# Row-wise largest magnitude of an 8192 x 8192 matrix: 64 adjacent rows per partition and one store at the end

## The chip, the cores and the metric

One core of one Trainium2 chip runs the kernel. The metric is the device time of one execution in microseconds (us), lower is better. Repeated executions of the kernel before agree within 0.2%. Every timed comparison below uses fast runs (granted clock 1.0); single runs, whose state is unknown, are called that. Ratios are computed as the mean time of one kernel's fast runs over that of the other's of the same rounds, so they are not quite the ratio of the medians that are quoted.

## The reference

```python
def setup_inputs():
    return {"x": np.random.randn(8192, 8192).astype(np.float32)}   # 268.44 MB

def reference(x):
    return np.linalg.norm(x, ord=np.inf, axis=1)   # max |x| of each row, 8192 results
```

Each element is read once and takes part in one maximum. There is nothing to reuse, so the kernel is a stream of loads with a reduction behind it.

## The kernel before

The 8192 rows are dealt out to 128 partitions, 64 rows each, in 32 tiles of two rows per partition (8 MB a tile, 64 KB per partition). The first 24 tiles, the bulk, are each one load and one reduction on the vector engine (DVE). The last 8 tiles, the tail, are loaded in ever shorter column pieces, so that DVE can follow closely and little work is left after the last byte. A list fixes the pieces. Three tile buffers rotate; all loads are issued by SyncE (SP), on one queue.

```python
TAIL = [ [2944, 13440], [4096, 12288], [11520, 4864], [7680, 8704],   # columns of float32
    [6528, 3328, 6528], [4864, 4096, 3328, 4096], [3968, 3584, 3328, 2944, 2560],
    [2432, 2176, 1920, 1664, 1536, 1280, 1152, 1024, 1152, 1024, 1024] ]
# ... (cut: bookkeeping, and a hook that issues the first load early)
# G=4, B=2, P=128, A=6, W=2*8192; split = 6144 rows
x_b = x[:split].rearrange("(a p n b) c -> a n p (b c)", p=P, a=A, n=G, b=B)
out_b = out[:split].rearrange("(a p n b) -> p a (n b)", p=P, a=A, n=G, b=B)
x_t = x[split:].rearrange("(p t b) c -> t p (b c)", p=P, b=B)
out_t = out[split:].rearrange("(p t) -> p t", p=P)
# ...
for a in range(A):
    for n in range(G):
        t = sbuf.tile([P, W + PAD], F32, tag="t")
        nc.sync.dma_start(out=t[:, :W], in_=x_b[a, n])
        absmax(r_bulk[:, a, n*B:(n+1)*B], t[:, :W].rearrange("p (b c) -> p b c", b=B))
nc.scalar.dma_start(out=out_b, in_=r_bulk[:])          # early store of the bulk's results
# ... tail: one load per piece from x_t[i][:, at:at+w], one or two reductions per piece
nc.scalar.dma_start(out=out_t[:, :n_tail-1], in_=r_tail[:, :n_tail-1])   # near the end
# ...
nc.sync.dma_start(out=out_t[:, n_tail-1:], in_=r_fin[:])                 # last row
```

The distance in memory between what neighbouring partitions read for one tile is called the pitch. A row is 32 KB. In the bulk a partition owns G*B = 8 adjacent rows, so the pitch is 256 KB. In the tail it owns 16, so it is 512 KB. The contiguous piece that one partition reads in one load is called the run: 64 KB in the bulk, 52.5 KB down to 4 KB in the tail. In the trace each run is one packet, moved by one of the 16 DMA engines; a load lands when its last packet has arrived.

Of the kernel before, what the change touches and what calls it, by code (L numbers as in the profile page):

```python
# [1 line left out]
logging.getLogger("concourse").setLevel(logging.ERROR)  # L3

# [1 line left out]

# [4 lines left out]

F32 = mybir.dt.float32
X = mybir.AxisListType.X



TAIL = [
    [2944, 13440],
    [4096, 12288],
    [11520, 4864],  # L20
    [7680, 8704],
    [6528, 3328, 6528],
    [4864, 4096, 3328, 4096],
    [3968, 3584, 3328, 2944, 2560],
    [2432, 2176, 1920, 1664, 1536, 1280, 1152, 1024, 1152, 1024, 1024],
]


def segments(loads, cols):

    out, at = [], 0
    for i, w in enumerate(loads):
        end = at + w
        while at < end:
            r = at // cols
            to = min(end, (r + 1) * cols)
            out.append((i, r, at - r * cols, to - at))
            at = to
    return out


def start_first_load_early(nc):


    sp = mybir.EngineType.SP
    first, *rest = nc.main_func.blocks
    for block in rest:
        insts = block.instructions
        for i, ins in enumerate(insts):
            if ins.engine == sp and type(ins).__name__ == "InstDMACopy":  # L50
                assert not ins.sync_info.on_wait
                moved = insts[i]
                block.instructions = insts[:i] + insts[i + 1 :]
                head = first.instructions
                at = next(k for k, h in enumerate(head) if h.engine == sp)
                first.instructions = head[:at] + [moved] + head[at:]
                return


@with_exitstack  # L60
def kernel(
    ctx: ExitStack,
    tc: tile.TileContext,
    x: bass.AP,
    out: bass.AP,
    G: int = 4,
    B: int = 2,
    BUFS: int = 3,
    PAD: int = 16,
):  # L70
    nc = tc.nc
    P = nc.NUM_PARTITIONS
    rows, cols = x.shape
    W = B * cols


    n_tail = B * len(TAIL)
    n_bulk_rows = rows // P - n_tail
    assert n_bulk_rows % (G * B) == 0
    A = n_bulk_rows // (G * B)  # L80
    split = n_bulk_rows * P
    x_b = x[:split].rearrange("(a p n b) c -> a n p (b c)", p=P, a=A, n=G, b=B)
    out_b = out[:split].rearrange("(a p n b) -> p a (n b)", p=P, a=A, n=G, b=B)
    x_t = x[split:].rearrange("(p t b) c -> t p (b c)", p=P, b=B)
    out_t = out[split:].rearrange("(p t) -> p t", p=P)

    sbuf = ctx.enter_context(tc.tile_pool(name="sbuf", bufs=BUFS))
    outp = ctx.enter_context(tc.tile_pool(name="outp", bufs=1))

    segs = [segments(loads, cols) for loads in TAIL]  # L90
    count = {}
    for i, s in enumerate(segs):
        for _, r, _, _ in s:
            count[i * B + r] = count.get(i * B + r, 0) + 1
    n_last = count[n_tail - 1]
    k_max = max(count[r] for r in range(n_tail - 1))
    assert n_last - 1 <= PAD

    r_bulk = outp.tile([P, A, G * B], F32)
    r_tail = outp.tile([P, n_tail], F32)  # L100
    r_fin = outp.tile([P, 1], F32)
    part = outp.tile([P, n_tail - 1, k_max], F32)
    nc.vector.memset(part[:], 0.0)  # L103

    def absmax(o, i):
        nc.vector.reduce_max(out=o, in_=i, axis=X, apply_absolute_value=True)  # L106

    for a in range(A):
        for n in range(G):
            t = sbuf.tile([P, W + PAD], F32, tag="t")  # L110
            nc.sync.dma_start(out=t[:, :W], in_=x_b[a, n])
            absmax(
                r_bulk[:, a, n * B : (n + 1) * B],
                t[:, :W].rearrange("p (b c) -> p b c", b=B),
            )
    nc.scalar.dma_start(out=out_b, in_=r_bulk[:])

    seen = {}
    for i, loads in enumerate(TAIL):
        t = sbuf.tile([P, W + PAD], F32, tag="t")  # L120
        todo = segs[i]
        at = 0
        for j, w in enumerate(loads):
            nc.sync.dma_start(out=t[:, at : at + w], in_=x_t[i][:, at : at + w])  # L124
            at += w
            for _, b, c, n in [s for s in todo if s[0] == j]:
                r = i * B + b
                k = seen.get(r, 0)
                seen[r] = k + 1
                lo = b * cols + c  # L130
                if r < n_tail - 1:
                    absmax(part[:, r, k : k + 1], t[:, lo : lo + n])
                    if r == n_tail - 2 and k == count[r] - 1:

                        absmax(r_tail[:, : n_tail - 1], part[:])
                        nc.scalar.dma_start(
                            out=out_t[:, : n_tail - 1], in_=r_tail[:, : n_tail - 1]
                        )
                elif k < n_last - 1:
                    absmax(t[:, W + k : W + k + 1], t[:, lo : lo + n])  # L140
                else:

                    absmax(r_fin[:], t[:, lo : W + n_last - 1])
    nc.sync.dma_start(out=out_t[:, n_tail - 1 :], in_=r_fin[:])
    nc.at_finalize(start_first_load_early)


# [1 line left out]
_INS = ['x']  # L149
_OUTS = [((8192,), 'float32')]  # L150


# [23 lines left out]
```

## Time and profile before

| | before |
|---|---|
| time | 628.59 us, median of 3 runs (628.57 to 628.78) |
| load queue | 99.3% of the 16 DMA engines' span, 268.44 MB |
| DVE | 553.0 us busy, 88% |
| last reduction starts | 623.80 us |

The page of the kernel before, its 40 slices and its queue table (packets, MB, share of the engines' span):

```profile
DVE  0688998888988889888898888998889999999998
...
DMA  9999999999999999999999999999999999999997
GB/s 401 468 401 468 401 468 401 464 405 455 414 451 418 451 418 401 468 401 468 401 468 401 468 401 468 401 468 401 468 418 406 460 430 410 436 422 430 428 423 287
...
q1 hardware_dynamic: 8064, 268.44, 99.3%
```

The DMA engines are busy in every slice but the last. The swing between 401 and 468 is only how long packets fall into slices; the windows view of the same kernel (stretch, its length, DVE busy time with instruction count, POOL, clock, DMA share, GB/s), in five stages, is flat in the bulk:

```profile
0.00:80.00 80.00, 51.80 (x5) 0.20 (x4) 1.00 1.01 433
80.00:480.00 400.00, 357.21 (x21) 0.00 (x0) 1.00 1.00 433
480.00:560.00 80.00, 79.28 (x14) 0.00 (x0) 1.00 0.99 426
560.00:600.00 40.00, 39.77 (x13) 0.00 (x0) 1.00 1.00 425
600.00:627.00 27.00, 24.95 (x15) 0.00 (x0) 1.00 0.84 350
```

The packet records in the trace say the same more sharply. A 64 KB packet nearly always takes 2.418 us, 27.1 GB/s on each of 16 engines, 434 GB/s in all. The Trainium skill, "DMA: Bandwidth & Descriptors", section "Where 436 GB/s comes from", gives 435.2 GB/s as the ceiling of the engines' ports; this trace agrees. Only the first 16 packets, which all start together, average 2.98 us.

The timeline of DVE in the kernel before (start, duration, what, and in brackets the idle time before it and what ended it):

```profile
21.93 17.22 DVE L106 TENSOR_REDUCE r_bulk<-t 128x2 f32<-128x16384 f32 x1 [20.95 <-DMA t<-in_x_dram]
41.22 17.22 DVE L106 TENSOR_REDUCE r_bulk<-t 128x2 f32<-128x16384 f32 x1 [2.07 <-DMA t<-in_x_dram]
60.58 17.22 DVE L106 TENSOR_REDUCE r_bulk<-t 128x2 f32<-128x16384 f32 x1 [2.14 <-DMA t<-in_x_dram]
...
615.73 0.22 DVE L106 TENSOR_REDUCE r_tail<-part 128x15 f32<-128x60 f32 x1
615.86 7.90 DVE L106 TENSOR_REDUCE t<-t 128x1 f32<-128x1536 f32 x6
623.80 1.23 DVE L106 TENSOR_REDUCE r_fin<-t 128x1 f32<-128x1030 f32 x1
```

In the bulk a tile arrives every 19.35 us, DVE needs 17.22 us for it and waits about 2 us for the next. In the tail DVE has a single gap, of 0.64 us. The start of each bulk reduction is therefore a clock for the loads: comparing it between two kernels shows where a loss arises. That is the main instrument below.

### The profile page before, as it was taken

Reading aid. Unit: us, or ns where it says so; the run is one execution under the profiler, and the core shown is the slowest. Engines: PE = TensorE matmul, PEld = TensorE weight load, DVE = VectorE, ACT = ScalarE, POOL = GpSimd, SP = SyncE. Lnnn points to the kernel's source line nnn. Section 1 sums busy time; section 2 is a strip of 40 time slices with the busy share of each in tenths; the row PEclk is TensorE's granted clock in tenths of the full one; section 3 lists DMA queues with packets and bytes.
Section 4 is the critical chain, followed back from the end, with each engine's and each line's share of the span. In section 5 each row is a group of like instructions: output and inputs, shape, how many; then the busy total and the mean of one; then the engine's idle time right before and its main releaser. Section 6 shows DMA issues by size and latency. Waiting matters only on the chain.

```text
span 627.3 us, 201 instructions
## 1 busy us (share of the span) xinstructions
DVE 553.0 (88%) x64; POOL 0.2 (0%) x4
## 2 busy tenths in 40 slices
DVE  0688998888988889888898888998889999999998
POOL 0000000000000000000000000000000000000000
DMA  9999999999999999999999999999999999999997
GB/s 401 468 401 468 401 468 401 464 405 455 414 451 418 451 418 401 468 401 468 401 468 401 468 401 468 401 468 401 468 418 406 460 430 410 436 422 430 428 423 287
DMA packets 8994, 268.49 MB, mean 428 GB/s; under 512 B 1952, under 2 KB 1952, under 8 KB 3104
## 3 DMA queue, kind: packets, MB, share of 16 engines
q1 hardware_dynamic: 8064, 268.44, 99.3%
q10 hardware_dynamic: 928, 0.03, 0.1%
q14 instruction: 2, 0.02, 0.0%
HBM read 268.44 MB, written 0.03 MB: 428 GB/s over the span
## 4 chain that ended last, share of the span: by engine, by line
DMA 67%; DVE 28%; another core or an unknown queue 4%; SPq 0%; issue 0%
DMA t<-in_x_dram 67%; DVE r_bulk L106 22%; DVE part L106 5%; DVE t L106 1%; DVE r_fin L106 0%; SPq L124 0%; DVE r_tail L106 0%
## 5 line engine op out<-in xcount | busy, mean ns | idle before, releaser
L106 DVE TENSOR_REDUCE r_bulk<-t 128x2 f32<-128x16384 f32 x24 | 413.3, 17220 | 70.1 <-DMA t<-in_x_dram 70.1
L106 DVE TENSOR_REDUCE part<-t 128x1 f32<-128x8192 f32 (+18 forms) x31 | 130.5, 4273 | 0.9 <-DMA t<-in_x_dram 0.6
L106 DVE TENSOR_REDUCE t<-t 128x1 f32<-128x1152 f32 (+3 forms) x6 | 7.9, 1387 | 0.0
L106 DVE TENSOR_REDUCE r_fin<-t 128x1 f32<-128x1030 f32 x1 | 1.2, 1226 | 0.0
L103 DVE MEMSET part<- 128x60 f32 x1 | 0.1, 108 | 0.9 <-PEq L160 0.9
L106 DVE TENSOR_REDUCE r_tail<-part 128x15 f32<-128x60 f32 x1 | 0.2, 216 | 0.0
L160 POOL MEMSET const-bfloat16-1.0<- 128x1 bf16 x1 | 0.1, 103 | 0.0
L160 POOL MEMSET const-uint8-127<- 128x1 uint8 x1 | 0.1, 103 | 0.0
L160 POOL MEMSET const-float32-1.0<- 128x1 f32 x1 | 0.1, 100 | 0.0
L160 POOL MEMSET const-float32-0.0<- 128x1 f32 x1 | 0.1, 99 | 0.2 <-issue 0.2
## 6 DMA issues: line engine op xcount, KB each, us to landing
t<-in_x_dram SPq DMA_DIRECT2D x1, 6720.0 KB, 40.4
t<-in_x_dram SPq DMA_DIRECT2D x2, 3264.0 KB, 26.4
t<-in_x_dram SPq DMA_DIRECT2D x3, 2048.0 KB, 29.0
t<-in_x_dram SPq DMA_DIRECT2D x1, 6144.0 KB, 40.6
t<-in_x_dram SPq DMA_DIRECT2D x1, 5760.0 KB, 35.3
t<-in_x_dram SPq DMA_DIRECT2D x3, 1664.0 KB, 32.5
t<-in_x_dram SPq DMA_DIRECT2D x2, 2432.0 KB, 32.6
t<-in_x_dram SPq DMA_DIRECT2D x1, 4352.0 KB, 42.8
```

The lines of the kernel that those rows point to most:

```text
L103: nc.vector.memset(part[:], 0.0)
L106: nc.vector.reduce_max(out=o, in_=i, axis=X, apply_absolute_value=True)
L160: nc = _bacc.Bacc("TRN2", target_bir_lowering=False, num_devices=1)
```

## The change

The intent is a simpler layout: every partition holds 64 adjacent rows throughout, so bulk and tail share one view, and each partition's 64 results are contiguous in the output. One store of 256-byte runs replaces three stores of short runs (768 of 32 bytes, 128 of 60, 128 of 4). The same rearrangement sets the pitch to 64 x 32 KB = 2 MB everywhere. Loads, their sizes and their order, and the reductions stay as they were.

```diff
-    x_b = x[:split].rearrange("(a p n b) c -> a n p (b c)", p=P, a=A, n=G, b=B)
-    out_b = out[:split].rearrange("(a p n b) -> p a (n b)", p=P, a=A, n=G, b=B)
-    x_t = x[split:].rearrange("(p t b) c -> t p (b c)", p=P, b=B)
-    out_t = out[split:].rearrange("(p t) -> p t", p=P)
+    x_v = x.rearrange("(p t b) c -> t p (b c)", p=P, b=B)
+    out_v = out.rearrange("(p t) -> p t", p=P)
 ...
-    r_bulk = outp.tile([P, A, G * B], F32)
-    r_tail = outp.tile([P, n_tail], F32)
-    r_fin = outp.tile([P, 1], F32)
+    res = outp.tile([P, n_rows], F32)
 ...
-            nc.sync.dma_start(out=t[:, :W], in_=x_b[a, n])
+        nc.sync.dma_start(out=t[:, :W], in_=x_v[i])
 ...
-    nc.scalar.dma_start(out=out_b, in_=r_bulk[:])
 ...
-            nc.sync.dma_start(out=t[:, at : at + w], in_=x_t[i][:, at : at + w])
+            nc.sync.dma_start(out=t[:, at : at + w], in_=x_v[n_bulk + i][:, at : at + w])
 ...
-                        nc.scalar.dma_start(out=out_t[:, : n_tail - 1], in_=r_tail[:, : n_tail - 1])
 ...
-    nc.sync.dma_start(out=out_t[:, n_tail - 1 :], in_=r_fin[:])
+    nc.sync.dma_start(out=out_v, in_=res[:])
```

More of the change, by code (lines that the diff above doesn't have):

```diff
@@ L65 @@
     out: bass.AP,
-    G: int = 4,
     B: int = 2,
@@ L74 @@
     W = B * cols
-    n_tail = B * len(TAIL)
-    n_bulk_rows = rows // P - n_tail
-    assert n_bulk_rows % (G * B) == 0
-    A = n_bulk_rows // (G * B)
-    split = n_bulk_rows * P
-    x_b = x[:split].rearrange("(a p n b) c -> a n p (b c)", p=P, a=A, n=G, b=B)
-    out_b = out[:split].rearrange("(a p n b) -> p a (n b)", p=P, a=A, n=G, b=B)
-    x_t = x[split:].rearrange("(p t b) c -> t p (b c)", p=P, b=B)
-    out_t = out[split:].rearrange("(p t) -> p t", p=P)
+    n_rows = rows // P
+    n_bulk = n_rows // B - len(TAIL)
+    first = n_bulk * B
+    last = n_rows - 1
+    x_v = x.rearrange("(p t b) c -> t p (b c)", p=P, b=B)
+    out_v = out.rearrange("(p t) -> p t", p=P)
     sbuf = ctx.enter_context(tc.tile_pool(name="sbuf", bufs=BUFS))
@@ L93 @@
         for _, r, _, _ in s:
-            count[i * B + r] = count.get(i * B + r, 0) + 1
-    n_last = count[n_tail - 1]
-    k_max = max(count[r] for r in range(n_tail - 1))
+            r += first + i * B
+            count[r] = count.get(r, 0) + 1
+    n_last = count[last]
+    k_max = max(n for r, n in count.items() if r < last)
     assert n_last - 1 <= PAD
-    r_bulk = outp.tile([P, A, G * B], F32)
-    r_tail = outp.tile([P, n_tail], F32)
-    r_fin = outp.tile([P, 1], F32)
-    part = outp.tile([P, n_tail - 1, k_max], F32)
+    res = outp.tile([P, n_rows], F32)
+    part = outp.tile([P, last - first, k_max], F32)
     nc.vector.memset(part[:], 0.0)
@@ L106, in absmax @@
         nc.vector.reduce_max(out=o, in_=i, axis=X, apply_absolute_value=True)
-    for a in range(A):
-        for n in range(G):
-            t = sbuf.tile([P, W + PAD], F32, tag="t")
-            nc.sync.dma_start(out=t[:, :W], in_=x_b[a, n])
-            absmax(
-                r_bulk[:, a, n * B : (n + 1) * B],
-                t[:, :W].rearrange("p (b c) -> p b c", b=B),
-            )
-    nc.scalar.dma_start(out=out_b, in_=r_bulk[:])
+    for i in range(n_bulk):
+        t = sbuf.tile([P, W + PAD], F32, tag="t")
+        nc.sync.dma_start(out=t[:, :W], in_=x_v[i])
+        absmax(
+            res[:, i * B : (i + 1) * B],
+            t[:, :W].rearrange("p (b c) -> p b c", b=B),
+        )
     seen = {}
@@ L123 @@
         for j, w in enumerate(loads):
-            nc.sync.dma_start(out=t[:, at : at + w], in_=x_t[i][:, at : at + w])
+            nc.sync.dma_start(
+                out=t[:, at : at + w], in_=x_v[n_bulk + i][:, at : at + w]
+            )
             at += w
             for _, b, c, n in [s for s in todo if s[0] == j]:
-                r = i * B + b
+                r = first + i * B + b
                 k = seen.get(r, 0)
@@ L130 @@
                 lo = b * cols + c
-                if r < n_tail - 1:
-                    absmax(part[:, r, k : k + 1], t[:, lo : lo + n])
-                    if r == n_tail - 2 and k == count[r] - 1:
-                        absmax(r_tail[:, : n_tail - 1], part[:])
-                        nc.scalar.dma_start(
-                            out=out_t[:, : n_tail - 1], in_=r_tail[:, : n_tail - 1]
-                        )
+                if r < last:
+                    absmax(part[:, r - first, k : k + 1], t[:, lo : lo + n])
+                    if r == last - 1 and k == count[r] - 1:
+                        absmax(res[:, first:last], part[:])
                 elif k < n_last - 1:
@@ L141 @@
                 else:
-                    absmax(r_fin[:], t[:, lo : W + n_last - 1])
-    nc.sync.dma_start(out=out_t[:, n_tail - 1 :], in_=r_fin[:])
+                    absmax(res[:, last:], t[:, lo : W + n_last - 1])
+    nc.sync.dma_start(out=out_v, in_=res[:])
     nc.at_finalize(start_first_load_early)
```

## The prediction

> **What bounds the kernel now.** DMA: the page shows 9 tenths busy in every slice but the last; its queue table gives the load queue 99.3% of the 16 DMA engines' span for 268.44 MB, 428 GB/s. The windows view reads 434 GB/s, DMA share 1.00, from 100 to 460 us. In the trace's packet records nearly every 65,536-byte load packet takes 2.42 us (27.1 GB/s per engine), as flat as an engine at its own limit, not at memory's. DVE is second: 17.22 us per 8 MB tile (groups by form), against about 19.3 us of DMA (half the period in the chain of waits). In the bulk DVE idles 70 us, all on loads; from 506 us to the end at 625 it runs without a gap.
>
> **What changes on the engines.** The order comparison shows the same DVE instructions, shapes and loads. Removed: two ACT stores (768 runs of 32 bytes, 128 of 60 bytes). The last store grows from 128 runs of 4 bytes to 128 of 256.
> - In 500:560, where the bulk store trickles, loads run at 425 instead of 434 GB/s: at most 1.2 us of DMA time (estimate: 2% of 60 us). DVE has no gap there and sets the end, so I credit under 0.5 us.
> - Last store: 1.4 us to landing now (issues table). A 256-byte run at 27 GB/s is about 10 ns, 8 per engine: below +0.3 us (estimate).
> - Alone this is a draw.
>
> **What moves: the address.** A bulk tile's partitions were 256 KB apart, the tail's 512 KB; now all are 2 MB apart. Tail packets of 46 and 54 KB still run at 27.1 GB/s per engine: no loss at 512 KB. The Trainium skill, "DMA: Bandwidth & Descriptors", section "Latency and other measured facts", row on HBM row pitch, gives copies of 128-partition tiles 207 GB/s per direction at a 512 KiB pitch, 164 at 2 MiB, 103 at 4 MiB, and guesses at channel aliasing of lock-stepped streams. No run here shows that yet. Those were copies with 16 KB rows; this is loads alone with 64 KB rows, so the loss may be smaller, or vanish when engines drift apart.
>
> **On the critical path:** all of it. Estimate from that page: 616 us of transfer (268.44 MB at 435 GB/s) times 207/164 is 778 us, plus start and end of about 10: 788. DVE then waits for each load, so its backlog at the end (about 5 us after the last landing) shrinks to about 1.5 us. I take three quarters of the effect: load packets average about 2.9 us.
>
> **Predicted: 745 us, 80% range 627 to 835. Faster by over 2%: 0.02; within 2%: 0.21; slower: 0.77.** Two humps: near 628 (no aliasing) and 680 to 820.
>
> **What would show it.** Right: 64 KB load packets longer than 2.42 us and uneven; load rate 340 to 400 GB/s at DMA share 1.0; DVE busy time still 553 us with far larger idle on loads, in the tail too; loads in the bulk landing after about 48 us instead of 40.7; DVE's last reduction within about 2 us of the last landing; last store about 1.5 us.
> Wrong: packets stay at 2.42 us; then the time is 628 within 1 us.
>
> **What would make it wrong.** Engines that drift apart after the first packets (here the first 16 take about 2.9 us, later ones 2.42) and so never meet on one memory channel; aliasing that hits stores more than loads; or a much stronger loss for loads alone, beyond 835.

## The result, and the profile after

| | before | after |
|---|---|---|
| time, median of 5 runs | 628.68 us (628.57 to 629.10) | 654.73 us (652.79 to 655.43) |
| ratio of fast runs | | 1.0407, 95% interval 1.0389 to 1.0424 |
| DVE busy | 553.0 us | 554.2 us |
| last reduction starts | 623.80 us | 647.98 us |

The changed kernel is slower by 26 us. That lies inside the stated range, in the gap between its two humps, but the forecast was a loss of about 117 us. The page of the changed kernel, the same lines:

```profile
DVE  0479888889888889988888988888989999999856
...
DMA  9999999999999999999999999999999999999994
GB/s 370 342 414 427 427 431 435 447 422 435 431 451 414 439 435 447 418 435 439 447 418 427 447 431 427 435 447 427 417 438 433 428 425 430 409 413 405 346 242 142
...
q1 hardware_dynamic: 8064, 268.47, 98.6%
```

The rate is low in the first two slices and in the last four, and as good as before between. DMA stays busy all the while, so it is the packets that take longer. The windows view of the changed kernel, by the same stages:

```profile
0.00:80.00 80.00, 46.48 (x4) 0.20 (x4) 1.00 0.99 395
80.00:480.00 400.00, 354.67 (x22) 0.00 (x0) 1.00 1.00 433
480.00:560.00 80.00, 79.22 (x13) 0.00 (x0) 1.00 1.00 429
560.00:600.00 40.00, 39.03 (x11) 0.00 (x0) 1.00 1.00 412
600.00:650.00 50.00, 34.78 (x18) 0.00 (x0) 1.00 0.86 256
```

The timeline of DVE in the changed kernel, at its start and end:

```profile
25.95 17.22 DVE L102 TENSOR_REDUCE res<-t 128x2 f32<-128x16384 f32 x1 [24.97 <-DMA t<-in_x_dram]
47.96 17.22 DVE L102 TENSOR_REDUCE res<-t 128x2 f32<-128x16384 f32 x1 [4.79 <-DMA t<-in_x_dram]
68.07 17.22 DVE L102 TENSOR_REDUCE res<-t 128x2 f32<-128x16384 f32 x1 [2.89 <-DMA t<-in_x_dram]
...
621.78 2.69 DVE L102 TENSOR_REDUCE part<-t 128x1 f32<-128x2432 f32 x1 [2.49 <-DMA t<-in_x_dram]
626.75 2.42 DVE L102 TENSOR_REDUCE part<-t 128x1 f32<-128x2176 f32 x1 [2.28 <-DMA t<-in_x_dram]
...
647.98 1.23 DVE L102 TENSOR_REDUCE res<-t 128x1 f32<-128x1030 f32 x1
```

Subtract the starts of the reductions before from those after: +4.0, +6.7, +7.5, +7.8 us for the first four, then 7.3 to 7.9 for the other twenty. The last reduction is +24.2. So the start loses 7.9 us in four tiles, the remaining bulk loses nothing at the same 2 MB pitch, and the tail loses 16.3 us (24.2 minus 7.9). The mean of the 64 KB packets, tile by tile, is 2.89, 2.66, 2.50, 2.43 us and then 2.42.

The stores cost nothing that shows: the last store is issued at 625.05 and 649.23 us, and the spans end 2.3 us later both times.

Two things are to be explained: why the 2 MB pitch costs at the start and then stops, and why it costs again in the tail.

### The profile page after: what moved, and what is told of

Its sections match the earlier page's. It is cut to its first block, busy times and chain, and to the rows that moved or that the text cites. A ratio compares the mean times of both kernels' runs of the same rounds, so it can differ in the third digit from the quotient of the medians.

```text
span 651.5 us, 197 instructions
## 1 busy us (share of the span) xinstructions
DVE 554.2 (85%) x64; POOL 0.2 (0%) x4
## 3 DMA queue, kind: packets, MB, share of 16 engines
HBM read 268.44 MB, written 0.03 MB: 412 GB/s over the span
## 4 chain that ended last, share of the span: by engine, by line
DMA 72%; DVE 27%; another core or an unknown queue 0%; issue 0%; SPq 0%
DMA t<-in_x_dram 72%; DVE res L102 24%; DVE part L102 3%; DVE t L102 0%; SPq L118 0%
## 5 line engine op out<-in xcount | busy, mean ns | idle before, releaser
L102 DVE TENSOR_REDUCE res<-t 128x2 f32<-128x16384 f32 (+1 forms) x25 | 414.5, 16580 | 78.0 <-DMA t<-in_x_dram 78.0
```

The costliest lines, as they stand in the source:

```text
L102: nc.vector.reduce_max(out=o, in_=i, axis=X, apply_absolute_value=True)
```

## The experiments

Theory A: the pitch is the whole cause, the stores cost nothing. Its refinement A1: engines collide when they read, at the same moment, at nearly the same offset modulo the pitch. They start in step and drift apart. Drifting apart helps only while a run is long enough to spread 16 engines over it. Rival A2: only starting together costs. Rival S: the store's new time is the cause. Rival D: any large distance between partitions costs.

"Wrong on purpose" below means that a kernel reads the same number of bytes in the same pieces (but for the small loads of section 7), some rows twice and others not, to move one address pattern alone. Losses by stage are read as above, against the profile of the kernel before. Each comes from one profiled run.

### 1. The two halves of the change

Changed addresses, old stores:

```diff
-    res = outp.tile([P, n_rows], F32)
+    res = outp.tile([P, first], F32)        # and r_tail, r_fin of their own
+    nc.scalar.dma_start(out=out_v[:, :first], in_=res[:])            # after the bulk
+    nc.scalar.dma_start(out=out_v[:, first:last], in_=r_tail[:])     # near the end
-    nc.sync.dma_start(out=out_v, in_=res[:])
+    nc.sync.dma_start(out=out_v[:, last:], in_=r_fin[:])
```

> The changed kernel's addresses with the three stores of the kernel before. Theory A (the 2 MB pitch costs the time, the stores nothing): 652 to 656 us, with the first three bulk tiles late by about 8 us and the tail by about 16 us. Rival S (the single late store, or the loss of the early one, costs it): about 629 us.

Measured: 658.76 us (4 runs, 656.94 to 661.41), ratio 1.0478. The bulk lost 10.0 us, all but 0.5 of it in the first four tiles, and the tail 20.0.

Old addresses, late stores:

```diff
-    nc.scalar.dma_start(out=out_b, in_=r_bulk[:])     # after the bulk
-    nc.scalar.dma_start(out=out_t[:, :n_tail-1], in_=r_tail[:, :n_tail-1])
-    nc.sync.dma_start(out=out_t[:, n_tail-1:], in_=r_fin[:])
+    nc.scalar.dma_start(out=out_b, in_=r_bulk[:])     # at the very end
+    nc.sync.dma_start(out=out_t, in_=r_tail[:])       # at the very end
```

> The addresses of the kernel before, with its early stores moved to the very end (two stores there, because its results lie in two places). Theory A: 628.5 to 630 us, at most 1.5 us over before for a second, larger store at the end. Rival S: 640 us or more.

Measured: 628.55 us, ratio 0.9997 (0.9982 to 1.0012). S falls: the time of the stores is worth nothing either way.

The first of these runs lay slightly above its expectation, 4 us above the changed kernel's own time, but it was measured in another session, on another chip. So the changed kernel was run again, unedited:

> The changed kernel again, unedited, on the chip of these runs, because the run with early stores (658.8 us) was slower than the changed kernel's first measurement (654.7 us) on another chip. If the chip or the draw of the engines' timing makes that difference: anything from 652 to 662 us here. If early stores cost 4 us under this pitch: 653 to 655 us.

Measured: 657.53 us (654.91 to 659.91), ratio 1.0452, with 9.7 us lost in the bulk and 19.6 in the tail. The loss varies by some us from run to run and from call to call, while the kernel before stays within 1 us. The 4 us were that variation; early stores need not be blamed.

### 2. Is it the distance, or the same offset?

The pitch becomes 2 MB minus 4 KB and nothing else changes (wrong on purpose).

```diff
-    x_v = x.rearrange("(p t b) c -> t p (b c)", p=P, b=B)
+    pitch = n_rows * cols - 1024
+    x_f = x.rearrange("r c -> (r c)")[: P * pitch].rearrange("(p s) -> p s", p=P)
+    # tile i is x_f[:, lo : lo + W] with lo = min(i * W, pitch - W)
```

> The changed kernel with a pitch of 2 MB minus 4 KB between partitions and nothing else changed (a wrong result on purpose: rows are shifted by up to 508 KB). Theory A in the form of aliasing at equal offsets: about 628.7 us, second reduction starting near 41.2 us and last near 623.8 us, as in before. Rival: any large distance between partitions costs (for example many memory pages at once): 650 us or more.

Measured: 631.26 us (629.73 to 633.70), ratio 1.0041 (1.0015 to 1.0066). Its second and last reduction (before: 41.22 and 623.80):

```profile
41.46 17.22 DVE L108 TENSOR_REDUCE res<-t 128x2 f32<-128x16384 f32 x1 [2.33 <-DMA t<-in_x_dram]
624.42 1.23 DVE L108 TENSOR_REDUCE res<-t 128x1 f32<-128x1030 f32 x1
```

The first four tiles are late by 0 to 0.5 us, the last reduction by 0.6 us. The profile is of the fastest of the four runs; over all of them 2.4 us are left (631.26 against 628.85). Moving each partition by 4 KB more than its neighbour, two thousandths of the distance, takes away nearly all the loss. D falls. The Trainium skill, "DMA: Bandwidth & Descriptors", section "Latency and other measured facts", row on HBM row pitch, advises padding by a few KiB; this run agrees.

### 3. The threshold

Pitches of 1 MB and 512 KB, with correct results and one late store:

```diff
-    x_v = x.rearrange("(p t b) c -> t p (b c)", p=P, b=B)
-    out_v = out.rearrange("(p t) -> p t", p=P)
+    S = 2      # 1 MB; S = 4 for 512 KB
+    x_v = x.rearrange("(s p t b) c -> s t p (b c)", s=S, p=P, b=B)
+    out_v = out.rearrange("(s p t) -> p s t", s=S, p=P)
```

> A pitch of 1 MB, correct result, one late store. Theory A does not fix the threshold; from the copies in the Trainium skill's table (207 GB/s at 512 KiB, 164 at 2 MiB) 1 MB should lose between nothing and half of what 2 MB loses: 629 to 642 us. Rival S: about 655 us, since the store is as late.

(The table it names is the row on HBM row pitch that the prediction cites.)

Measured: 641.65 us (641.17 to 642.51), ratio 1.0207. The bulk lost 12.6 us, 9.9 of it in the first four tiles and the rest in single later ones; the tail lost nothing (11.9 us late at the end).

> A pitch of 512 KB everywhere, correct result, one late store. The tail of the kernel before already runs at 512 KB without loss, so if bulk and tail obey one threshold the whole is 628.5 to 630 us. If the start from lock-step has its own threshold (1 MB lost 12.6 us in the bulk and nothing in the tail), the bulk may still lose some: 630 to 640 us with the loss in the first four tiles only.

Measured: 629.36 us, ratio 1.0009 (0.9995 to 1.0024). No loss anywhere. So the two losses have different thresholds: the start loses at 1 MB and 2 MB, the tail only at 2 MB.

### 4. Start and tail apart

Bulk at 256 KB with the tail at 2 MB, then the reverse (both wrong on purpose):

```diff
-        nc.sync.dma_start(out=t[:, :W], in_=x_v[i])
+        nc.sync.dma_start(out=t[:, :W], in_=x_b[i // 4, i % 4])   # x_b: the bulk view of before
```

> Bulk loads at 256 KB, tail loads at 2 MB, one late store (a wrong result on purpose: the two parts overlap in rows). If start and tail lose independently: no loss in the bulk, about 16 to 20 us in the tail, 645 to 649 us. If the tail's loss is a consequence of what the bulk left behind: about 629 us.

Measured: 653.74 us (651.89 to 656.05), ratio 1.0399. Nothing lost in the bulk, 24.5 us in the tail, more than expected. The window at 480:560, where the tail's pieces are still long, reads 412 GB/s here against 429 in the changed kernel:

```profile
480.00:560.00 80.00, 73.70 (x14) 0.00 (x0) 1.00 0.99 412
```

The 52.5 KB packets of the tail average 2.35 us here, 2.02 in the changed kernel and 1.99 before. So long runs lose once more at their first meeting with the 2 MB pitch, as at the start. That the engines came from the bulk still in step (section 7 has the measure: their starts lay within 0.90 us, against 1.60 in the changed kernel) would explain it; this was not tested apart.

```diff
-                out=t[:, at : at + w], in_=x_v[n_bulk + i][:, at : at + w]
+                out=t[:, at : at + w], in_=x_t[i][:, at : at + w]   # x_t: the tail view of before
```

> Bulk loads at 2 MB, tail loads at 512 KB, one late store (a wrong result on purpose). If the two lose independently: about 8 to 10 us in the first four tiles, nothing in the tail, 637 to 640 us.

Measured: 639.41 us (637.29 to 643.46), ratio 1.0177. 10.2 us lost in the bulk (8.9 in the first four tiles), nothing in the tail. Each loss comes from the pitch of its own part, but they do not simply add: 10.2 and 24.5 make more than the 24 to 30 of the whole.

### 5. The length of a run

A ladder replaces bulk and tail: 32 tiles, each loaded whole or in equal pieces, and reduced whole.

```diff
+    widths = [16384]*7 + [8192]*6 + [4096]*6 + [2048]*6 + [1024]*6 + [16384]
+    for i, w in enumerate(widths):
+        t = sbuf.tile([P, W + PAD], F32, tag="t")
+        for at in range(0, W, w):
+            nc.sync.dma_start(out=t[:, at : at + w], in_=src(i)[:, at : at + w])
+        absmax(res[:, i*B:(i+1)*B], t[:, :W].rearrange("p (b c) -> p b c", b=B))
```

(`src(i)` is tile i at the pitch in question.)

> All 32 tiles at 2 MB, cut into loads of 64, 32, 16, 8 and 4 KB per partition, seven tiles at 64 KB and six at each other size (then one last at 64 KB), correct result. Theory A1 (engines collide when their addresses modulo the pitch lie within a few KB of each other, so drifting apart helps only while a run is long enough to spread 16 engines over it): the load rate falls with the run, about 434 GB/s at 64 and 32 KB after the start, about 400 at 16 KB, 300 at 8 KB and 200 or less at 4 KB. Theory A2 (only starting together costs, run length does not matter): 434 GB/s falling only to about 410 at 4 KB, which is what the packet durations of 4 KB in before give.

> The same ladder at a pitch of 256 KB, the control for the number of loads and the length of a packet. A1 and A2 both: 434 GB/s down to 16 KB, about 420 at 8 KB, about 405 to 412 at 4 KB. If 4 KB loads are slow here too (issue on SP takes about 0.35 us and 4 KB for 128 partitions needs 1.2 us of DMA), the loads' number would be to blame and not the pitch.

> The ladder at 2 MB minus 4 KB (a wrong result on purpose). A1: as the control at 256 KB at every run length, within 2%. If short runs far apart are slow for another reason (many distant places per microsecond): as slow as the ladder at 2 MB.

Each was one run: 809.33 us at 2 MB, 654.28 us at 256 KB and 654.32 us at 2 MB minus 4 KB (before: 629.59). The windows view of the ladder at 2 MB, one row per run length, from 64 KB down to 4 KB, each cut where the last tile of its length had arrived:

```profile
0.00:150.90 150.90, 103.36 (x7) 0.20 (x4) 1.00 0.99 398
150.90:267.30 116.40, 103.28 (x6) 0.00 (x0) 1.00 1.00 432
267.30:394.10 126.80, 103.37 (x7) 0.00 (x0) 1.00 0.99 396
394.10:581.00 186.90, 103.27 (x7) 0.00 (x0) 1.00 1.00 270
581.00:768.60 187.60, 103.31 (x6) 0.00 (x0) 1.00 1.02 273
```

The same view of the ladder at 256 KB:

```profile
0.00:138.30 138.30, 103.32 (x6) 0.20 (x4) 1.00 1.00 428
138.30:254.90 116.60, 103.36 (x7) 0.00 (x0) 1.00 1.00 432
254.90:372.00 117.10, 103.28 (x6) 0.00 (x0) 1.00 1.01 430
372.00:490.90 118.90, 103.35 (x7) 0.00 (x0) 1.00 1.01 424
490.90:612.90 122.00, 103.30 (x6) 0.00 (x0) 1.00 1.03 416
```

Worked out from the starts of the reductions, the mean time of a tile is:

| run | 2 MB | 256 KB | 2 MB - 4 KB |
|---|---|---|---|
| 64 KB | 20.65 us (22.7, 21.6, 21.1, then 19.5) | 19.38 | 19.66 |
| 32 KB | 19.41 | 19.42 | 19.41 |
| 16 KB | 21.12 | 19.53 | 19.52 |
| 8 KB | 31.16 | 19.81 | 19.74 |
| 4 KB | 31.27 | 20.34 | 20.26 |

A2 falls: at 2 MB short runs lose all the time, long after the start. The number of loads is not to blame, since the other two ladders issue just as many. The 4 KB padding removes the loss at every length. The fall with the run length is as A1 has it, except that 4 KB is no worse than 8 KB: 269 GB/s at 8 KB and 268 at 4 KB (8.389 MB over 31.16 and 31.27 us), a floor, where 300 and 200 or less were expected.

This sizes the tail. Its last tile comes in runs of 4 to 9.5 KB, which should cost about 11 us (31.2 minus 20); the one before it, 10 to 15.5 KB, between 1.6 and 11; the one before that, 13 to 19 KB, about 1.6. That is an estimate of 14 to 24 us, and the tail lost 16.3 and 19.6.

### 6. The tail with long runs

```diff
-TAIL = [ [2944, 13440], ... ]
+TAIL = [[16384]] * 8
```

> The changed kernel with each of the eight tail tiles loaded whole, 64 KB per partition (DVE then ends a tile's reductions later, so its own end is worse). A1: only the start's loss is left against the same tail at the pitches of before, 8 to 10 us. If the tail loses for another reason than short runs: 22 us or more.

> The kernel before with its tail loaded whole: the control. DMA ends as before near 620 us, DVE needs about 17 us after the last landing: about 640 us.

Measured: 651.61 us at 2 MB and 644.00 us at the pitches of before. The control is 4 us slower than I expected, which was not pursued; the difference of the two, 7.6 us (expected: 8 to 10), is what tells. In the profiles the 2 MB kernel is 6.0 us late at the end of the bulk against before, its control 0.4 early, and the last reductions stand 6.3 us apart, first the 2 MB kernel, then its control:

```profile
645.01 0.16 DVE L93 TENSOR_REDUCE res<-part 128x15 f32<-128x15 f32 x1
638.74 0.16 DVE L97 TENSOR_REDUCE r_tail<-part 128x15 f32<-128x15 f32 x1
```

With 64 KB runs the tail at 2 MB loses nothing. The tail's loss is the short runs.

### 7. The start: in step, or cold?

To start the engines apart, the first tile was read at 2 MB minus 4 KB, where nothing is lost, and small loads were put behind it, each to fewer engines than the last. This is wrong on purpose in the first tile's rows. The first attempt used 15 small loads:

```diff
+        return x_p[:, :W] if i == 0 else x_v[i]      # x_p: the view at 2 MB minus 4 KB
 ...
+        if i == 0:
+            d = sbuf.tile([P, W + PAD], F32, tag="t")
+            for j, k in enumerate(range(15, 0, -1)):
+                nc.sync.dma_start(out=d[:k, j*1024:(j+1)*1024], in_=x_v[8][:k, :1024])
```

> The changed kernel, but its first tile is read at 2 MB minus 4 KB, and behind it come 15 small loads of 4 KB per engine to 15, 14, ... 1 engines, so that each engine starts its first 2 MB tile about 0.18 us after its neighbour, 2.7 us in all (a wrong result on purpose, in the first tile's rows only). If it is the starting together that costs the 8 to 10 us in the bulk: the last bulk reduction starts about 2 to 4 us later than in before, which is the small loads themselves. If being in step does not matter: 9 to 13 us later. The tail should lose 16 to 20 us either way under A1.

One run, 660.81 us (before: 629.59); the last bulk reduction 14.9 us late. It failed as a test. The view of the SP queue's waits shows 20.3 us of waiting by a small load on the first tile's landing, so the engines ran dry and met again.

The second attempt used six small loads, and a control gave three to all engines:

```diff
+            for j, k in enumerate([15, 13, 11, 8, 5, 2]):     # control: [16] * 3
+                nc.sync.dma_start(out=d[:k, j*2048:(j+1)*2048], in_=x[:k, :2048])
```

> As the failed run with 15 small loads, but with six (8 KB per engine, to 15, 13, 11, 8, 5 and 2 engines, from adjacent rows), few enough that the queue should not wait: seven groups of engines enter the first 2 MB tile 8 KB apart, 1.8 us from first to last (a wrong result on purpose in the first tile's rows). If starting in step costs the bulk its 8 to 10 us: the last bulk reduction starts 1 to 4 us later than in before. If not: 9 to 12 us later. The tail should lose 16 to 20 us more either way.

> The control: three small loads of 8 KB to all 16 engines instead, the same bytes within a tenth, no engine ahead of another. If starting in step costs: the last bulk reduction starts 9 to 12 us later than in before (0.9 us of it the small loads). If the first tile's other pitch alone takes the loss away: 1 to 3 us.

Measured: 655.15 us staggered (651.27 to 657.11), 656.01 us control (655.70 to 659.37). In the total they are not apart. The last bulk reduction came 11.3 us late staggered and 12.1 in the control. By the numbers written down beforehand the staggered run thus falls into the branch in which being in step does not matter (9 to 12 us). What speaks for lock-step is the reading by tiles, made after the result and from one profile of each. The timeline of the staggered kernel, the second to sixth bulk reduction:

```profile
48.80 17.22 DVE L108 TENSOR_REDUCE res<-t 128x2 f32<-128x16384 f32 x1 [6.93 <-DMA t<-in_x_dram]
68.34 17.22 DVE L108 TENSOR_REDUCE res<-t 128x2 f32<-128x16384 f32 x1 [2.32 <-DMA t<-in_x_dram]
87.68 17.22 DVE L108 TENSOR_REDUCE res<-t 128x2 f32<-128x16384 f32 x1 [2.12 <-DMA t<-in_x_dram]
107.29 17.22 DVE L108 TENSOR_REDUCE res<-t 128x2 f32<-128x16384 f32 x1 [2.39 <-DMA t<-in_x_dram]
126.65 17.22 DVE L108 TENSOR_REDUCE res<-t 128x2 f32<-128x16384 f32 x1 [2.13 <-DMA t<-in_x_dram]
```

The same of the control:

```profile
46.87 17.22 DVE L108 TENSOR_REDUCE res<-t 128x2 f32<-128x16384 f32 x1 [4.49 <-DMA t<-in_x_dram]
69.37 17.22 DVE L108 TENSOR_REDUCE res<-t 128x2 f32<-128x16384 f32 x1 [5.28 <-DMA t<-in_x_dram]
89.81 17.22 DVE L108 TENSOR_REDUCE res<-t 128x2 f32<-128x16384 f32 x1 [3.22 <-DMA t<-in_x_dram]
110.41 17.22 DVE L108 TENSOR_REDUCE res<-t 128x2 f32<-128x16384 f32 x1 [3.38 <-DMA t<-in_x_dram]
130.90 17.22 DVE L108 TENSOR_REDUCE res<-t 128x2 f32<-128x16384 f32 x1 [3.27 <-DMA t<-in_x_dram]
```

From the second to the sixth reduction the staggered kernel takes 77.85 us, 19.5 a tile; the control takes 84.03, 21.0 a tile, losing 6.6 us more against before while the other loses 0.5. The third tile's packets average 2.43 us staggered and 2.78 in the control. The second tile, the first at 2 MB, is no better staggered (2.72 us against 2.71), but the packet records part there too. Staggered, each engine's first packet, which started while the small loads were still running, took up to 7.1 us; from its second packet on, the means of 16 are 2.42 to 2.47 us, with the 16 starts spread over 2.4 us. In the control the starts lie within 1.2 us; its second and third packets still take 2.42 us, and the means of the thirteen rounds after them are 2.49 to 3.04. So engines whose starts are spread over a whole packet ran at full rate once the small loads were through; engines closer together lost for five tiles, after a full tile at another pitch, so it is not a cold memory. One difference is not ruled out: the third tile's load was issued at 27.3 us in the control and at 41.9 staggered; from 42.5 us on both had the same loads queued, and they still differ. The expectation of 1 to 4 us in all failed on the small loads, which were slow themselves (8 KB took up to 1.45 us instead of 0.31), and the second tile lost about 5 us. The staggered kernel also crept from 9.1 to 11.3 us late in the last tiles of the bulk.

The drift itself can be worked out from the packet records: sort the starts of 16 successive packets modulo 2.418 us, take the shortest arc that holds them, and average over the eight groups of a tile. (Where packets differ in length this is rough.) In the kernel before, the arc is 0.8 us in the first tiles and narrows to 0.7, so the engines do not drift apart by themselves there. In the changed kernel it is 1.4 us in the first tile and 1.6 from the fourth on; in the control 0.8 in the first tile, at the other pitch, and 1.8 from the seventh on. In the staggered kernel it is 1.8 in the seventh tile but narrows to 0.8 in the 22nd, while the mean packet goes from 2.42 us to 2.51 in the 23rd. The creep is thus what A1 expects of engines that come back together, though why they do is open; in the run of section 4 with only the bulk at 2 MB an arc of 1.1 us did no harm.

The last two runs take the ladder upwards, from 4 KB to 64 KB:

```diff
-    widths = [16384]*7 + [8192]*6 + [4096]*6 + [2048]*6 + [1024]*6 + [16384]
+    widths = [1024]*6 + [2048]*6 + [4096]*6 + [8192]*6 + [16384]*8
```

> The ladder upwards at 1 MB: six tiles each at 4, 8, 16 and 32 KB per run, then eight at 64 KB, correct result. If a start in step costs whatever the run: the first tiles at 4 KB are slow (360 to 390 GB/s). If short runs are immune at 1 MB and only long ones in step lose: 412 GB/s at 4 KB as in the control, and a loss of several us at 32 or 64 KB, late in the kernel, where the engines are still in step.

> The ladder upwards at 2 MB. Short runs: about 268 GB/s at 4 and 8 KB and 397 at 16 KB, from the start, as when taken downwards. If short runs put the engines back in step, the first tiles at 32 or 64 KB lose again (20 to 22 us for a tile instead of 19.35) near 500 us, so that a cold start is not the cause; if the loss at the start was a cold start, they take 19.35 us.

At 1 MB (658.94 us, one run, before 628.57): the first reduction starts at 24.51 us against 21.93 in before (22.04 in the 256 KB ladder), the second tile takes 22.6 us, and from the third on the 4 KB runs are at 19.9 to 20.6, as in the control. Later only the first three tiles at 64 KB lose again, 20.1, 20.3 and 19.6. So at 1 MB a start in step costs about 5 us even with short runs, which then run free: the first expectation holds in the main, and a little of the second.

At 2 MB (808.76 us): 257, 270 and 403 GB/s at 4, 8 and 16 KB, from the start. The first two tiles at 32 KB take 20.3 us each and the first at 64 KB 20.9, then 19.3 to 19.8. About 4 us are lost again, more than 500 us after the kernel's start, where the start itself cost 6 to 12 with 64 KB runs (the least in the kernel with the whole tail, the most in the ladder at 2 MB). A cold start can't do that; short runs that put the engines partly back in step would.

## Why the prediction was wrong

- **Direction, place and bound: right.** The pitch of the loads is the cause, and all of it lies on the critical path. DMA stayed at a share of 0.99 to 1.00 until 600 us, DVE's busy time stayed (554.2 us) and its idle time on loads grew, in the tail from 0.6 to 15.9 us.
- **The stores: right.** They are a draw: moving them alone gives a ratio of 0.9997, and the last store took 1.5 us to land.
- **The step that failed: "616 us of transfer (268.44 MB at 435 GB/s) times 207/164 is 778 us", of which I took "three quarters of the effect: load packets average about 2.9 us".** I charged a rate from copies with 16 KB runs to every byte. In fact the term has two small parts. About three quarters of the bytes pay next to nothing: 20 of the 32 tiles are the bulk after its first four, with packets at 2.42 us, and the tail's first four tiles have long runs. The bulk's packets averaged 2.45 us in place of 2.9, and the kernel's loads 412 GB/s in place of 340 to 400. The start costs 7.9 to 9.7 us and the tail 16.3 to 19.6 us, in place of 117. The prediction said itself that the copies had 16 KB rows and these loads 64 KB, but took off only a quarter for it, for every stage alike. The ladder answers what the length of a run does: at 2 MB, 432 GB/s with 32 KB runs, 397 with 16 KB and 269 with 8 KB (8.389 MB over each mean time of a tile). Even at the copies' own 16 KB the loads lost 8% (397 against 430 GB/s at 256 KB), not the 21% that the term 207/164 stands for.
- **"Engines that drift apart after the first packets": named, and given too little weight.** The bulk behaved so: its loss ended after four tiles. The prediction gave a hump near 628 for it but did not see that it would act in one stage and not in another, nor that the way to tell was in its own profile: which stage has long runs and which has short ones.
- **Loads in the bulk landing after 48 us: wrong**, the median was 40.8, for the same reason.
- **A backlog of "about 5 us after the last landing" to be given back: wrong.** In the kernel before the last loads were issued at 613.7 us and no load of that stage landed in less than 9.9 us, so the last one landed no earlier than 623.6 (its last packet ended at 623.3), just before the last reduction at 623.80. There was no backlog to give back.

What stays open: that the addresses and the length of the runs cause the loss is shown; that engines in step collide at equal offsets (A1) is inferred from addresses and times, since no record here shows the memory's channels. Why the tail is free at 1 MB while the start is not, what sets the floor of 268 GB/s, and why the small loads took four times as long, were not settled. No kernel tried here is faster than the one before.

## What to carry to other kernels

When a layout puts partitions 1 MB or 2 MB apart (no larger pitch was run), look at the length of each partition's contiguous run as well as at the pitch: at 2 MB, runs of 32 KB and more lost mainly in the first tiles after a start or a change of pitch or of run length, and runs of 8 KB and less ran at 62% of full rate all the time (269 against 434 GB/s). Keep the pitch at 256 or 512 KB, or shift it by 4 KB as was done here at 2 MB, and be most careful with short pieces at the end of a kernel. And before multiplying a rate into all the bytes, split the kernel into stages and ask which of them meets the conditions under which the rate was measured.

## What the Trainium skill lacked or had wrong

- "DMA: Bandwidth & Descriptors", section "Latency and other measured facts", row on HBM row pitch: it gives one rate for each pitch, from copies with 16 KiB rows, and doesn't say what the length of a run does. For loads alone at 2 MB the runs here show 432 GB/s at 32 KB, 397 at 16 KB, 269 at 8 KB and 268 at 4 KB, and full rate at 64 KB after the first four tiles.
- The same row has no figure for 1 MB: the bulk lost 12.6 us there, 9.9 of it in the first four tiles (641.65 us in all), and the short runs of the tail nothing.
- The same row calls aliasing of streams in lock-step an inference. The staggered run supports the lock-step part, by one profile of each and without a gain in total time: 19.5 us a tile when engines enter apart, 21.0 when they enter closer together, at the same addresses.
- No page says that the loss fades by itself with long runs: packets of 64 KB went from 2.89 to 2.42 us within four tiles.
- The page's padding of a few KiB is right here also with a minus sign: 2 MB minus 4 KB gave 631.26 us against 654.73 to 657.53.
